# State space tables from compact operands, rotation first, one latent normalization later in the list, and a shorter exponential polynomial

## Chip, cores and metric

The kernel runs on one core of a Trainium2 chip. The metric is the device time of one execution in microseconds (us), the median of several runs. TensorE (PE in the rows) multiplies matrices, VectorE (DVE), ScalarE (ACT) and GpSimd (POOL) work on elements, and SyncE (SP) issues nearly all transfers. Each engine takes its instructions strictly in the order of its own queue, so an instruction that waits holds up everything behind it on that engine.

## What is computed

A trunk of two layers over 256 tokens of width 1024. Each layer has three token mixers in parallel (RWKV-7, latent attention, a diagonal state space model called S5), a gated merge, and a SwiGLU feed-forward network, each followed by a layer norm. The change touches the S5 parameters, which depend on the weights alone:

```python
step = exp(log_step); mag = exp(lam_re * step); ang = lam_im * step
lb_re, lb_im = mag * cos(ang), mag * sin(ang)          # lambda
f_re, f_im = (lambda - 1) / lam                        # complex
bb = f * b                                             # complex, 32 groups x 64 states x 16 channels
bu = einsum('btgc,gpc->btgp', ug, bb)
s  = associative_scan(lambda, bu)                      # over 256 positions
y  = Re(einsum('btgp,gcp->btgc', s, c)) + d_skip * u
```

and the normalization of the two latent vectors of the attention, `rms_norm(c_q)` and `rms_norm(c_kv)`, of layer 0.

## The kernel before

All projections are computed in three passes of a split format: each weight chunk (128 x 1024 fp32) is loaded by SyncE into a tile `raw` (3 buffers), cast by ScalarE to its high part (`whi`, line 161), and VectorE computes the low part (`wlo`, line 171; for a few chunks GpSimd does the last columns, line 173). There are 4 buffers of each part, and four chunks are kept ahead of the one in use. A projection unit uses two chunks: 48 matmuls on lines 203 to 205.

The work of a layer's first stage is written as a list of tokens, `ORDER1`. For layer 0: `S0 S1` are the S5 input projections, `m` the latents, `P` parameter loads, `r0` to `r6` the RWKV projections, `G1 to G3` gate projections, `T0 T1 T2` the parts of the S5 tables, `N` the latent normalization (`mla_norm`, lines 619 to 651), `t0` to `t3` with `w0` to `w3` the four S5 tiles, `g0 g1` the activation after them. The list order is not the queue order: a scheduler of the framework puts every instruction into its engine's queue by its own estimate of when its operands are there, and uses the list as a priority. So an instruction of a late token can stand early in a queue when an engine would otherwise be free.

The S5 scalars come from line 262 on, on VectorE in tiles of 128 x 32: `exp_acc` (line 275) evaluates an exponential with 24 instructions, and is called for `step` and for the magnitude. Sine and cosine come from ScalarE (lines 309, 310).

`s5_tables` (line 348) is a generator in three parts:
- T0 (to the first `yield`): loads of `pb` (line 362, the B operand) and `cd` (line 376, the C operand) from `in_spB`, in which the host has stored them already spread to block-diagonal form, half zeros. Then three complex products `cmul` (lines 379 to 386, six instructions of 128 x 512 each): B times f, B times lambda, C times minus conjugate lambda, and a negation (line 394).
- T1: 32 transposes of `bd` into `bl` (line 404) and 32 small matmuls for `k0` (line 413).
- T2: the rotation tables `ct` and `st` (lines 421 to 435), cos and sin of n times the angle for 128 steps, by doubling: 12 blocks of six instructions, from 128 x 16 elements each up to 128 x 512.

In layer 0 the products run on VectorE and the rotation on GpSimd (`TE_ = "VG"`). The tables of layer 1 are made during the first feed-forward matmuls of layer 0, all on GpSimd, at the units f = 7, 12 and 17 (`TAB_AT`).

An S5 tile (`s5_tile`, line 693) multiplies a matmul result (line 702, weights `bl`) with `ct` and `st` on VectorE (lines 709 to 712), scans (line 721), multiplies again (lines 725 to 727), and finishes on TensorE (lines 735 to 747).

The normalization `N` squares and sums on ScalarE (lines 624, 625), adds the epsilon on VectorE (line 235), takes the power -1/2 on GpSimd (line 237, tile `rsm`), and scales on ScalarE (lines 630, 631):

```python
def rsqrt(out, in_, eps, E=V):
    if eps:
        E.tensor_scalar(out=out, in0=in_, scalar1=eps, scalar2=None, op0=ALU.add)
        in_ = out
    G.tensor_tensor(out=out, in0=in_, in1=mh(out), op=ALU.pow)
```

After the feed-forward matmuls of layer 0 comes `token_major` (line 474), which loads `lg`, `lb` and `xk` (lines 493 to 495) into memory that the temporary tiles of `s5_tables` held before.

Of the kernel before, what the change touches and what calls it, by code (L numbers as in the profile page):

```python
# [26 lines left out]
    "S0 m S1 P r0 T0 T1 r1 N T2 r2 t0 w0 r3 G3 t1 t2 w1 r4 r5 w2 t3 w3 g0 G1 r6 G2 g1",  # L27
# [6 lines left out]
TAB_AT = (7, 12, 17)  # L34
# [52 lines left out]
def trunk(ctx: ExitStack, tc: tile.TileContext, xT, xtok, ws, spA, spB, spC, sp5, lnv, cst, out, dbg=None,  # L87
# [181 lines left out]
    with tc.tile_pool(name="s5set", bufs=1) as q:  # L269
# [78 lines left out]
    def s5_tables(l, tab, tmp, G, E):  # L348
# [12 lines left out]
        pb = tmp.tile([128, 2, 8, 2, 32], F32, name="pb", tag="pb")  # L361
        SY.dma_start(out=pb, in_=spB[l, :, 0:1024].rearrange("p (r q a c) -> p r q a c", r=2, q=8, a=2))
# [8 lines left out]
        G.tensor_tensor(out=st[:, :, 0], in0=cc, in1=cc, op=ALU.add)  # L371

        bd = tmp.tile([128, 8, 2, 2, 2, 32], F32, name="bd", tag="bd")
        bt = tmp.tile([128, 8, 2, 32], F32, name="bt", tag="bt")
        cd = tab.tile([128, 4, 8, 2, 32], F32, name="cd", tag="cd")
        SY.dma_start(out=cd[:, 0:2], in_=spB[l, :, 1024:2048].rearrange("p (r q a c) -> p r q a c", r=2, q=8, a=2))
        sh4 = [128, 8, 2, 32]

        def cmul(o_re, o_im, fr, fi, x_re, x_im):
            fr, fi = bc(v2(fr, 8).unsqueeze(3), sh4), bc(v2(fi, 8).unsqueeze(3), sh4)  # L380
            G.tensor_tensor(out=o_re, in0=x_re, in1=fr, op=ALU.mult)
            G.tensor_tensor(out=bt, in0=x_im, in1=fi, op=ALU.mult)
            G.tensor_tensor(out=o_re, in0=o_re, in1=bt, op=ALU.subtract)
            G.tensor_tensor(out=o_im, in0=x_im, in1=fr, op=ALU.mult)
            G.tensor_tensor(out=bt, in0=x_re, in1=fi, op=ALU.mult)
            G.tensor_tensor(out=o_im, in0=o_im, in1=bt, op=ALU.add)

        def B(i, ri):
            return bd[:, :, ri, :, i]

        cmul(B(1, 0), B(1, 1), s5fr[:, p0:p0 + 16], s5fi[:, p0:p0 + 16], pb[:, 0], pb[:, 1])
        cmul(B(0, 0), B(0, 1), lr, li, B(1, 0), B(1, 1))

        G.tensor_scalar(out=cd[:, 1], in0=cd[:, 1], scalar1=-1.0, scalar2=None, op0=ALU.mult)
        G.tensor_scalar(out=li, in0=li, scalar1=-1.0, scalar2=None, op0=ALU.mult)
        cmul(cd[:, 2], cd[:, 3], lr, li, cd[:, 0], cd[:, 1])
# [3 lines left out]
        for q4 in range(4):  # L400
            ps = mxps("a")
            for qq in range(2):
                for ri in range(2):
                    PE.transpose(ps[:, 256 * qq + 128 * ri:256 * qq + 128 * ri + 128],
                                 bd[:, 2 * q4 + qq, ri].rearrange("p a i c -> p (a i c)"), ident)
# [12 lines left out]
        yield  # L418
        mark("s5pre")

        t2 = tmp.tile([128, 16, 32], F32, name="t2", tag="t2")
        n = 1
        while n < 128:
            w = min(n, 32)
            lc, ls = (bc(x[:, :, n - 1:n], [128, 16, w]) for x in (ct, st))
            for o in range(0, n, w):
                c0, s0, t = ct[:, :, o:o + w], st[:, :, o:o + w], t2[:, :, 0:w]
                c1, s1 = ct[:, :, n + o:n + o + w], st[:, :, n + o:n + o + w]
                E.tensor_tensor(out=c1, in0=c0, in1=lc, op=ALU.mult)
                E.tensor_tensor(out=t, in0=s0, in1=ls, op=ALU.mult)  # L430
                E.tensor_tensor(out=c1, in0=c1, in1=t, op=ALU.subtract)
                E.tensor_tensor(out=s1, in0=c0, in1=ls, op=ALU.mult)  # L432
                E.tensor_tensor(out=t, in0=s0, in1=lc, op=ALU.mult)
                E.tensor_tensor(out=s1, in0=s1, in1=t, op=ALU.add)  # L434
            n *= 2
# [84 lines left out]
    for l in range(layers):  # L520
# [136 lines left out]
        with tc.tile_pool(name=f"s5p{l}", bufs=1, side=P) as q:  # L657
# [831 lines left out]
```

## Time and profile before

| | |
|---|---|
| median of 3 runs | 1088.11 us (1084.67 to 1090.08) |
| the profiled execution | 1090.58 us, its span 1088.9 us |
| mean granted TensorE clock | 0.972 |
| PE busy | 1026.9 us, 94% of the span |
| DVE busy | 802.8 us, 74% |
| ACT busy | 477.3 us, 44% |
| POOL busy | 231.5 us, 21% |

A row of a timeline gives the start, the duration, the engine, the line, the operation, output and inputs, and in brackets the idle time of the engine before it with what ended it. Times are from the start of the span. Matmuls overlap, so how fast TensorE really goes is read from how many of them start in a stretch, not from the duration of one.

### The profile page before, as it was taken

How to read it: one execution, taken by the hardware profiler on the slowest of the kernel's cores; microseconds unless marked ns; L12 is line 12 of the kernel's file. 1: busy time of each engine (PE TensorE's matmuls, PEld its weight loads, DVE VectorE, ACT ScalarE, POOL GpSimd, SP SyncE). 2: the span in 40 equal slices, each digit the busy share in tenths (PEclk: the TensorE clock that was granted, in tenths of full speed). 3: DMA queues.
4: the chain of work that ended last, by engine and by line, in shares of the span. 5: the costliest groups of instructions: out<-in, count | busy, mean ns of one | idle time of the engine just before them, and what ended most of it. 6: DMA issues, size and time to landing. Idle time of an engine off the chain costs nothing.

```text
span 1088.9 us, 21216 instructions
## 1 busy us (share of the span) xinstructions
PE 1026.9 (94%) x8560; PEld 923.8 (85%) x8560; DVE 802.8 (74%) x1560; ACT 477.3 (44%) x789; POOL 231.5 (21%) x254
## 2 busy tenths in 40 slices
PE   9489999999999999899998999999999899999997
PEld 8378887888897899798878999878889779999985
DVE  7599988977478799576473898789756866676645
ACT  5243387544343344244325345765334433434331
POOL 2941042210000599400011003221002420000000
PEclk9789999999999999999998899999999999999999
DMA  7342262132285655466545325222225746555552
GB/s 279 98 140 86 95 192 73 59 118 96 81 291 183 204 173 167 178 209 217 184 143 177 115 80 173 90 97 79 79 98 169 243 152 230 186 183 180 186 195 78
DMA packets 47683, 164.91 MB, mean 151 GB/s; under 512 B 5729, under 2 KB 8289, under 8 KB 46689
## 3 DMA queue, kind: packets, MB, share of 16 engines
q1 hardware_dynamic: 47296, 163.03, 45.2%
q8 instruction: 67, 1.10, 0.4%
q10 hardware_dynamic: 288, 0.52, 0.1%
q14 instruction: 32, 0.25, 0.1%
HBM read 157.77 MB, written 4.19 MB: 149 GB/s over the span
## 4 chain that ended last, share of the span: by engine, by line
PE 61%; DVE 17%; POOL 10%; DMA 5%; ACT 3%; issue 3%; SPq 0%; DVEq 0%; ACTq 0%; POOLq 0%
PE mm L205 11%; PE mm L204 11%; PE mm L203 11%; DMA raw<-in_ws 4%; PE mm L488 3%; PE mm L489 3%; PE mm L487 3%; DVE wlo L171 3%; ACT whi L161 2%; DVE z L721 2%; POOL st L432 1%; POOL st L434 1%; PE pa L702 1%; POOL t L430 1%; PE pa L916 1%
## 5 line engine op out<-in xcount | busy, mean ns | idle before, releaser
L171 DVE TENSOR_TENSOR wlo<-raw,whi 128x1024 fp32r<-128x1024 f32 (+2 forms) x265 | 336.7, 1277 | 175.3 <-ACT whi L161 173.2
L161 ACT CAST whi<-raw 128x1024 fp32r<-128x1024 f32 (+2 forms) x267 | 277.5, 1043 | 386.0 <-PE mm L204 207.3
L203 PE MATMUL mm<-xh,whi 128*128 128x256 f32 x1312 | 379.5, 289 | 14.2 <-ACT whi L161 14.1
L205 PE MATMUL mm<-xh,wlo 128*128 128x256 f32 x1312 | 378.3, 289 | 2.1 <-DVE wlo L171 1.9
L204 PE MATMUL mm<-xl,whi 128*128 128x256 f32 x1312 | 379.3, 289 | 0.4 <-DVE xl L259 0.4
L203 PEld LDWEIGHTS mm<-xh,whi 128*128 128x128 f32 x1312 | 252.5, 192 | 18.7 <-ACT whi L161 14.7
L205 PEld LDWEIGHTS mm<-xh,wlo 128*128 128x128 f32 x1312 | 253.5, 193 | 6.1 <-DVE wlo L171 2.9
L204 PEld LDWEIGHTS mm<-xl,whi 128*128 128x128 f32 x1312 | 252.4, 192 | 3.9 <-issue 1.8
L237 POOL TENSOR_TENSOR rs<-rs,mhalf 128x1 f32<-128x1 f32 x8 | 7.8, 970 | 344.0 <-DVE rs L235 344.0
L203 PE MATMUL mm<-yh,whi 128*128 128x256 f32 x256 | 74.5, 291 | 0.1
L205 PE MATMUL mm<-yh,wlo 128*128 128x256 f32 x256 | 74.1, 290 | 0.0
L204 PE MATMUL mm<-yl,whi 128*128 128x256 f32 x256 | 74.1, 289 | 0.0
L488 PE MATMUL mm<-wlo,hh 128*128 128x512 f32 x132 | 52.0, 394 | 0.0
L487 PE MATMUL mm<-whi,hh 128*128 128x512 f32 x132 | 51.6, 394 | 0.0
L489 PE MATMUL mm<-whi,hl 128*128 128x512 f32 x132 | 51.5, 393 | 0.0
L203 PEld LDWEIGHTS mm<-yh,whi 128*128 128x128 f32 x256 | 48.5, 189 | 2.3 <-ACT qa L113 0.9
L204 PEld LDWEIGHTS mm<-yl,whi 128*128 128x128 f32 x256 | 48.5, 189 | 1.2 <-issue 0.8
L205 PEld LDWEIGHTS mm<-yh,wlo 128*128 128x128 f32 x256 | 48.6, 190 | 1.1 <-issue 0.7
L173 POOL TENSOR_TENSOR wlo<-raw,whi 128x384 fp32r<-128x384 f32 (+2 forms) x24 | 29.5, 1236 | 72.4 <-ACT whi L161 72.4
L237 POOL TENSOR_TENSOR rsn<-rsn,mhalf 128x8 f32<-128x8 f32 x4 | 6.5, 1634 | 142.8 <-DVE rsn L235 142.8
L923 POOL TENSOR_SCALAR_AFFINE_SELECT Mk<-Mk 64x512 f32<-64x512 f32 x32 | 27.0, 844 | 43.6 <-ACT Mk L113 42.3
L487 PEld LDWEIGHTS mm<-whi,hh 128*128 128x128 f32 x132 | 24.8, 188 | 6.1 <-DVE th L1260 0.7
(498 smaller groups left out, 1764.2 us busy)
## 6 DMA issues: line engine op xcount, KB each, us to landing
raw<-in_ws SPq DMA_DIRECT2D x267, 512.0 KB, 4.1
raw<-in_ws SPq DMA_DIRECT2D x8, 416.0 KB, 3.5
xd<-xk SPq DMA_DIRECT2D x3, 1024.0 KB, 4.1
xk<-xd SPq DMA_DIRECT2D x3, 1024.0 KB, 7.9
lg<-in_lnv SPq DMA_DIRECT2D x4, 512.0 KB, 5.1
lb<-in_lnv SPq DMA_DIRECT2D x4, 512.0 KB, 5.7
pc<-in_spC SPq DMA_DIRECT2D x2, 768.0 KB, 5.1
pb<-in_spB SPq DMA_DIRECT2D x2, 512.0 KB, 5.2
```

The lines of the kernel that those rows point to most:

```text
L161: S.copy(out=hi[:, s], in_=raw[:, s])
L171: V.tensor_tensor(out=lo[:, 0:m], in0=raw[:, 0:m], in1=hi[:, 0:m].bitcast(F32), op=ALU.subtract)
L173: G.tensor_tensor(out=lo[:, m:w], in0=raw[:, m:w], in1=hi[:, m:w].bitcast(F32), op=ALU.subtract)
L203: PE.matmul(ps, lhsT=wh, rhs=xh, start=first, stop=False)
L204: PE.matmul(ps, lhsT=wh, rhs=xl, start=False, stop=False)
L205: PE.matmul(ps, lhsT=wl, rhs=xh, start=False, stop=last)
L237: G.tensor_tensor(out=out, in0=in_, in1=mh(out), op=ALU.pow)
L487: PE.matmul(acc[b][n], lhsT=ah, rhs=w[0][:, s], start=(k == 0), stop=False)
L488: PE.matmul(acc[b][n], lhsT=ah, rhs=w[1][:, s], start=False, stop=False)
L489: PE.matmul(acc[b][n], lhsT=al, rhs=w[0][:, s], start=False, stop=(k == nk - 1))
L721: V.tensor_tensor_scan(out=z[:, pp, qq, ri], data0=bc(m2[:, j:j + 1], [128, 128]), data1=z[:, pp, qq, ri], initial=0.0, op0=ALU.mult, op1= ...
L923: G.affine_select(out=Mk[r, h], in_=Mk[r, h], pattern=[[0, 4], [1, 2], [1, 64]], compare_op=ALU.is_ge, fill=0.0, base=-1, channel_multipli ...
```

## The change

The host stores the B and C operands compactly (16 columns for each group, no zeros), so one load of half the size replaces two. The complex products work in place on the compact tile `pb`, with six instructions of 128 x 256; a helper `spread` then writes the block-diagonal form with two ScalarE instructions of 128 x 512, each scaled with a 0/1 column. There are four spreads, so eight ScalarE instructions for each layer. The generator has five parts now. In layer 0 the rotation stands in the first; in layer 1 it stays last. `N` of layer 0 goes from behind `r1` to behind `r5`, `t0` from behind `r2` to behind `G3`. `exp_acc` has 15 instructions in place of 24.

```diff
-    "S0 m S1 P r0 T0 T1 r1 N T2 r2 t0 w0 r3 G3 t1 t2 w1 r4 r5 w2 t3 w3 g0 G1 r6 G2 g1",
+    "S0 m S1 P r0 T0 T1 r1 T2 T3 r2 r3 T4 G3 t0 w0 r4 t1 r5 N w1 t2 w2 r6 t3 w3 g0 G1 G2 g1",
...
-TAB_AT = (7, 12, 17)
+TAB_AT = (7, 8, 9, 12, 17)
...
-            V.tensor_scalar(out=xc, in0=src, scalar1=-104.0, scalar2=88.7, op0=ALU.max, op1=ALU.min)
+            V.tensor_scalar(out=xc, in0=src, scalar1=-88.1, scalar2=88.7, op0=ALU.max, op1=ALU.min)
             V.tensor_scalar(out=n, in0=xc, scalar1=1.4426950408889634, scalar2=MAGIC, op0=ALU.mult, op1=ALU.add)
-            V.tensor_scalar(out=n, in0=n, scalar1=MAGIC, scalar2=None, op0=ALU.subtract)
-            V.tensor_scalar(out=n, in0=n, scalar1=-127.0, scalar2=127.0, op0=ALU.max, op1=ALU.min)
+            V.tensor_scalar(out=n, in0=n, scalar1=MAGIC + 127.0, scalar2=MAGIC, op0=ALU.min, op1=ALU.subtract)
...
-            V.tensor_scalar(out=r, in0=r, scalar1=-1.0, scalar2=1.0, op0=ALU.max, op1=ALU.min)
             co = [1.0 / math.factorial(k) for k in range(9)]
-            V.tensor_scalar(out=pl, in0=r, scalar1=co[8], scalar2=co[7], op0=ALU.mult, op1=ALU.add)
-            for k in range(6, -1, -1):
-                V.tensor_tensor(out=pl, in0=pl, in1=r, op=ALU.mult)
-                V.tensor_scalar(out=pl, in0=pl, scalar1=co[k], scalar2=None, op0=ALU.add)
             V.tensor_scalar(out=ni, in0=n, scalar1=127.0, scalar2=8388608.0, op0=ALU.add, op1=ALU.mult)
-            V.tensor_tensor(out=dst, in0=pl, in1=ni.bitcast(F32), op=ALU.mult)
+            V.tensor_scalar(out=pl, in0=r, scalar1=co[8], scalar2=None, op0=ALU.mult)
+            for k in range(7, 0, -1):
+                V.scalar_tensor_tensor(out=pl, in0=pl, scalar=co[k], in1=r, op0=ALU.add, op1=ALU.mult)
+            V.scalar_tensor_tensor(out=dst, in0=pl, scalar=1.0, in1=ni.bitcast(F32), op0=ALU.add, op1=ALU.mult)
...
-        pb = tmp.tile([128, 2, 8, 2, 32], F32, name="pb", tag="pb")
-        SY.dma_start(out=pb, in_=spB[l, :, 0:1024].rearrange("p (r q a c) -> p r q a c", r=2, q=8, a=2))
+        pb = tmp.tile([128, 4, 8, 2, 16], F32, name="pb", tag="pb")
+        SY.dma_start(out=pb, in_=spB[l].rearrange("p (r q a c) -> p r q a c", r=4, q=8, a=2))
...
+        def rotation():
...
+        if first:
+            rotation()
+            yield
...
-        SY.dma_start(out=cd[:, 0:2], in_=spB[l, :, 1024:2048].rearrange("p (r q a c) -> p r q a c", r=2, q=8, a=2))
...
+        def cmul(x, fr, fi):
+            fr, fi = (bc(v2(t, 8).unsqueeze(3), [128, 8, 2, 16]) for t in (fr, fi))
+            G.tensor_tensor(out=bs, in0=x[:, 0], in1=fi, op=ALU.mult)
+            G.tensor_tensor(out=bt, in0=x[:, 1], in1=fi, op=ALU.mult)
+            G.tensor_tensor(out=x[:, 0], in0=x[:, 0], in1=fr, op=ALU.mult)
+            G.tensor_tensor(out=x[:, 1], in0=x[:, 1], in1=fr, op=ALU.mult)
+            G.tensor_tensor(out=x[:, 0], in0=x[:, 0], in1=bt, op=ALU.subtract)
+            G.tensor_tensor(out=x[:, 1], in0=x[:, 1], in1=bs, op=ALU.add)
+
+        def spread(dst, src):
+            for g in range(2):
+                S.activation(out=dst[:, :, 16 * g:16 * g + 16], in_=src.rearrange("p r q a c -> p (r q a) c"),
+                             func=AF.Identity, scale=C(f"g{g}"))
...
+        cmul(pb[:, 0:2], s5fr[:, p0:p0 + 16], s5fi[:, p0:p0 + 16])
+        spread(bdv[:, :, 1], pb[:, 0:2])
+        G.tensor_scalar(out=pb[:, 3], in0=pb[:, 3], scalar1=-1.0, scalar2=None, op0=ALU.mult)
+        spread(cd[:, 0:2].rearrange("p r q a c -> p (r q a) c"), pb[:, 2:4])
+        yield
+        cmul(pb[:, 0:2], lr, li)
+        spread(bdv[:, :, 0], pb[:, 0:2])
+        yield
         G.tensor_scalar(out=li, in0=li, scalar1=-1.0, scalar2=None, op0=ALU.mult)
-        cmul(cd[:, 2], cd[:, 3], lr, li, cd[:, 0], cd[:, 1])
+        cmul(pb[:, 2:4], lr, li)
+        spread(cd[:, 2:4].rearrange("p r q a c -> p (r q a) c"), pb[:, 2:4])
         yield
...
+        if not first:
+            yield
+            rotation()
```

In the diff `G` is the engine that `s5_tables` is given for the products: VectorE in layer 0, GpSimd in layer 1. The first call passes `first=True`, the second `False`.

## Rows read from the trace of the kernel before

**Rows 1.** The page: TensorE and its clock in 40 slices, tenths.
```profile
PE   9489999999999999899998999999999899999997
PEclk9789999999999999999998899999999999999999
```
**Rows 2.** Busy time by stretch: length, PE, PEld, DVE, ACT, POOL, PEclk, DMA share, GB/s.
```profile
34.20:46.20 12.00, 2.79 (x24) 2.58 (x22) 0.00 (x0) 1.73 (x4) 11.59 (x17) 0.76 0.01 4
46.20:67.90 21.70, 10.16 (x107) 9.09 (x108) 21.67 (x17) 5.74 (x12) 21.27 (x14) 0.66 0.32 97
...
97.00:134.00 37.00, 36.37 (x441) 32.10 (x440) 36.74 (x81) 12.97 (x20) 1.06 (x1) 1.00 0.26 88
...
36.90:71.20 34.30, 13.55 (x124) 12.39 (x124) 24.97 (x22) 8.58 (x17) 30.25 (x25) 0.65 0.21 63
455.00:470.00 15.00, 9.87 (x58) 9.37 (x58) 9.02 (x14) 6.44 (x9) 0.00 (x0) 0.77 0.73 258
...
56.90:60.70 3.80, 3.80 (x19) 3.80 (x19) 3.80 (x6) 0.47 (x1) 3.72 (x4) 0.50 0.34 130
...
380.00:400.00 20.00, 20.00 (x169) 20.00 (x169) 19.35 (x21) 8.32 (x12) 19.92 (x15) 1.00 0.58 181
```
**Rows 3.** Waits, 20 to 80 us: who waited for whom, total, times, longest.
```profile
ACT lt L630 <- POOL rsm L237: 14.6, 1, 14.6
...
PE mm L203 <- ACT whi L161: 9.3, 1, 9.3
...
PE pb L413 <- DVE bd L383: 7.3, 1, 7.3
```
**Rows 4.** Timeline of GpSimd: start of the rotation, the power, end of the rotation.
```profile
23.91 0.22 POOL L429 TENSOR_TENSOR ct<-ct 128x16 f32<-128x16 f32 x1 [3.59 <-DVE ct L369]
...
41.36 1.04 POOL L430 TENSOR_TENSOR t<-st 128x512 f32<-128x512 f32 x1
...
43.39 1.04 POOL L237 TENSOR_TENSOR rsm<-rsm,mhalf 128x4 f32<-128x4 f32 x1
...
66.25 1.61 POOL L434 TENSOR_TENSOR st<-st,t 128x512 f32<-128x512 f32 x1
```
**Rows 5.** Timeline of VectorE in layer 0's first stage.
```profile
14.10 0.19 DVE L289 TENSOR_TENSOR t5pl<-t5pl,t5r 128x32 f32<-128x32 f32 x1
14.33 0.18 DVE L290 TENSOR_SCALAR t5pl<-t5pl 128x32 f32<-128x32 f32 x1
...
65.16 1.56 DVE L383 TENSOR_TENSOR bd<-bd,bt 128x512 f32<-128x512 f32 x1
...
79.81 0.69 DVE L709 TENSOR_TENSOR pa__882<-pa,ct 128x512 f32<-128x512 f32 x1 [0.85 <-PE pa L702]
...
87.92 0.41 DVE L727 SCALAR_TENSOR_TENSOR pb<-z,st 128x256 f32<-128x256 f32 x1
```
**Rows 6.** VectorE's groups by shape, 380 to 450 us (GpSimd busy).
```profile
L171 DVE TENSOR_TENSOR wlo<-raw,whi 128x1024 fp32r<-128x1024 f32 x22 | 41.7, 1924 | 2.2 <-ACT whi L161 2.2
L1291 DVE TENSOR_TENSOR hl<-th,hh 128x256 fp32r<-128x256 f32 x11 | 12.5, 1141 | 0.4
```
**Rows 7.** The same groups, 470 to 500 us (GpSimd idle).
```profile
L171 DVE TENSOR_TENSOR wlo<-raw,whi 128x1024 fp32r<-128x1024 f32 x10 | 12.2, 1223 | 6.3 <-ACT whi L161 6.2
L1291 DVE TENSOR_TENSOR hl<-th,hh 128x256 fp32r<-128x256 f32 x6 | 2.5, 425 | 0.2
```
**Rows 8.** Timeline of GpSimd in layer 0's feed-forward stage: a step of 256, the last step.
```profile
382.23 0.61 POOL L430 TENSOR_TENSOR t<-st 128x256 f32<-128x256 f32 x1
...
447.12 2.15 POOL L434 TENSOR_TENSOR st<-st,t 128x512 f32<-128x512 f32 x1
```
**Rows 9.** SyncE's own waits, 360 to 500 us.
```profile
SPq L493 <- POOL st L434: 12.1, 1, 12.1
```
**Rows 10.** Timeline of ScalarE: a late cast, an activation with a column operand.
```profile
459.02 1.04 ACT L161 CAST whi<-raw 128x1024 fp32r<-128x1024 f32 x1 [13.99 <-DMA raw<-in_ws]
...
635.61 0.72 ACT L762 ACTIVATE ga<-ga,ones 128x512 f32<-128x512 f32 x1
```

More of the change, by code (lines that the diff above doesn't have):

```diff
@@ L346, in step, with s5_tables @@
             next(g)
-    def s5_tables(l, tab, tmp, G, E):
+    def s5_tables(l, tab, tmp, G, E, first):
         mark("s5pre")
@@ L371, in s5_tables @@
         G.tensor_tensor(out=st[:, :, 0], in0=cc, in1=cc, op=ALU.add)
-        bd = tmp.tile([128, 8, 2, 2, 2, 32], F32, name="bd", tag="bd")
-        bt = tmp.tile([128, 8, 2, 32], F32, name="bt", tag="bt")
-        cd = tab.tile([128, 4, 8, 2, 32], F32, name="cd", tag="cd")
-        SY.dma_start(out=cd[:, 0:2], in_=spB[l, :, 1024:2048].rearrange("p (r q a c) -> p r q a c", r=2, q=8, a=2))
[L377 to L394, printed above, removed]
+        def rotation():
+            mark("s5pre")
+            t2 = tmp.tile([128, 16, 32], F32, name="t2", tag="t2")
+            n = 1
+            while n < 128:
+                w = min(n, 32)
+                lc, ls = (bc(x[:, :, n - 1:n], [128, 16, w]) for x in (ct, st))
+                for o in range(0, n, w):
+                    c0, s0, t = ct[:, :, o:o + w], st[:, :, o:o + w], t2[:, :, 0:w]
+                    c1, s1 = ct[:, :, n + o:n + o + w], st[:, :, n + o:n + o + w]
+                    E.tensor_tensor(out=c1, in0=c0, in1=lc, op=ALU.mult)
+                    E.tensor_tensor(out=t, in0=s0, in1=ls, op=ALU.mult)
+                    E.tensor_tensor(out=c1, in0=c1, in1=t, op=ALU.subtract)
+                    E.tensor_tensor(out=s1, in0=c0, in1=ls, op=ALU.mult)
+                    E.tensor_tensor(out=t, in0=s0, in1=lc, op=ALU.mult)
+                    E.tensor_tensor(out=s1, in0=s1, in1=t, op=ALU.add)
+                n *= 2
@@ new lines, in s5_tables @@
+        if first:
+            rotation()
+            yield
+            mark("s5pre")
+        bt, bs = (tmp.tile([128, 8, 2, 16], F32, name=n, tag=n) for n in ("bt", "bs"))
+        bd = tmp.tile([128, 2, 8, 2, 2, 32], F32, name="bd", tag="bd")
+        cd = tab.tile([128, 4, 8, 2, 32], F32, name="cd", tag="cd")
+        def cmul(x, fr, fi):
[6 more added lines that the diff above has]
+            G.tensor_tensor(out=x[:, 1], in0=x[:, 1], in1=bs, op=ALU.add)
@@ L404, in s5_tables @@
                     PE.transpose(ps[:, 256 * qq + 128 * ri:256 * qq + 128 * ri + 128],
[L405 removed]
+                                 bd[:, ri, 2 * q4 + qq].rearrange("p a i c -> p (a i c)"), ident)
             cp(0, out=bl[:, 2 * q4:2 * q4 + 2], in_=ps.rearrange("p (q r s) -> p q r s", q=2, r=2))
@@ L412, in s5_tables @@
             for ri in range(2):
-                PE.matmul(o, lhsT=bd[:, qx, ri, pp, 1], rhs=cd[:, ri, qx, pp], start=(ri == 0), stop=(ri == 1),
+                PE.matmul(o, lhsT=bd[:, ri, qx, pp, 1], rhs=cd[:, ri, qx, pp], start=(ri == 0), stop=(ri == 1),
                           skip_group_check=True)
@@ L417, in s5_tables @@
             cp(1, out=k0[r], in_=v2(ps[r, 0:256], 8))
[L418 to L435, printed above, removed]
+        if not first:
+            yield
+            rotation()
         tb.update(ct=ct, st=st, m2=m2, cd=cd, bl=bl, k0=k0)
@@ L677, in s5_tables0 @@
                     tmps = ExitStack()
-                    tgen.append((tmps, s5_tables(0, tab, tmps.enter_context(tc.tile_pool(name="tmp0", bufs=1, side="right")), TE[0], TE[1])))
+                    tgen.append((tmps, s5_tables(0, tab, tmps.enter_context(tc.tile_pool(name="tmp0", bufs=1, side="right")), TE[0], TE[1], True)))
                 next(tgen[0][1])
-                if i == 2:
+                if i == 4:
                     tgen[0][0].close()
@@ L1293, in trunk @@
                     if f == TAB_AT[0]:
-                        gen = s5_tables(l + 1, tab, tmpq, G, G)
+                        gen = s5_tables(l + 1, tab, tmpq, G, G, False)
                     next(gen)
-                    if f == TAB_AT[2]:
+                    if f == TAB_AT[-1]:
                         tmpstack.close()
@@ L1439, in cb @@
             return a.reshape(16, 2, 16, 64).transpose(1, 3, 0, 2).reshape(128, 16, 16)
-        def diag(a):
-            o = np.zeros((2, 64, 16, 2, 16), np.float32)
-            for i in range(2):
-                o[i, :, :, i, :] = a.reshape(2, 64, 16, 16)[i]
-            return o.reshape(128, 512)
         cr, ci = cb(g["s5_c_re"][l]), cb(g["s5_c_im"][l])
-        spB.append(np.concatenate([diag(a) for a in (br, bi, cr, ci)], 1))
+        spB.append(np.concatenate([a.reshape(128, 256) for a in (br, bi, cr, ci)], 1))
     lre = np.concatenate([pg_(g["s5_lambda_re"][l]) for l in range(nl)], 1)
```

3 lines of the change are left out of this document (added).

## Prediction

> **What bounds the kernel now.** The page comes first: in its 40 slices TensorE shows nearly full digits everywhere but in the second (4, with the clock at 7), and 8 in the third, the 17th and the 22nd [rows 1]. The 22nd is the start of layer 1, which the change leaves as it is. So a gain has to come from the holes in the second and third and in the 17th slice; elsewhere a faster side engine buys nothing.
>
> The first hole is read by stretches [rows 2]. From 36.9 to 71.2 us TensorE is busy 13.6 of 34.3 us at a granted clock of 0.65, a mix of its two levels. From 34.2 to 46.2 VectorE does nothing at all, while GpSimd works 11.6 of 12 us. The waits name the chain [rows 3]: ScalarE stands 14.6 us at the scaling of the latents, behind the power on GpSimd; the weight casts queue behind it, so TensorE stands 9.3 us, then 7.3 us more for the table products, which VectorE could only start late. The power is one short instruction, but it stands in the middle of the rotation [rows 4]: GpSimd begins at 23.9, reaches the power at 43.4, and finishes the rotation at 67.9.
>
> The second hole is at 455 to 470 us. SyncE waits 12.1 us with its load of the norm's `lg` until GpSimd has finished the last step of layer 1's rotation at 449.3 [rows 8, 9], because that memory is still in use. Weight loads queue behind it; ScalarE then waits 14 us for a chunk [rows 10]. TensorE starts 58 matmuls in 15 us [rows 2]. At the upper clock level it starts one every 0.12 us (169 in 20 us) and at the lower one every 0.20 (19 in 3.8) [rows 2], so those 58 are 7 us of work: about 8 us are lost.
>
> **A shared resource.** A VectorE instruction with two operands in SBUF is lengthened while GpSimd runs, by a nearly fixed amount: 128 x 256 goes from 0.43 to 1.14 us, 128 x 1024 from 1.22 to 1.92 [rows 6, 7], and 128 x 512 from 0.69 in the S5 tile to 1.56 in a product [rows 5]. GpSimd's own step of 512 goes from 1.04 to 1.61 [rows 4]. From 46.2 to 67.9 the two take turns, 17 instructions against 14 [rows 2]. So I count the first hole as one shared queue: undisturbed, the 14 GpSimd steps are 14 x 1.04 = 14.6 us, and VectorE's 17 are about 11.0 (11 products at 0.69, two low parts at 1.15, four small ones); the sum, 25.6, took 21.7 us, a factor of 0.85. This matters: ending VectorE's 12 us of idleness does not bring 12 us, since GpSimd used that time undisturbed.
>
> **Polynomial.** Each call loses 9 of 24 instructions, which follow each other every 0.23 us [rows 5]: 2.1 us for each. The first sits before the rotation, so it starts at about 21.9, not 23.9; the second sits before the first product, so the products too can start about 2 us earlier. By the Vector Engine (DVE) Microarchitecture Reference of the Trainium skill (Points that are easy to get wrong) a scalar_tensor_tensor with two wide SBUF sources runs at half throughput; this would make each of the 16 new steps about 0.03 us longer and cost 0.5 us of the 4. The rows disagree: at 128 x 256 this form takes 0.41 us [rows 5], the plain one 0.43 [rows 7], so I leave it out.
>
> **Layer 0, products and rotation.** From 32.2 us on (34.2 less 2) GpSimd has left what it did in 34.2 to 46.2 without the power, 10.6 us, and 14.6 us: 25.2. VectorE must bring, up to the state that it had reached at 79.8, when the first S5 tile began [rows 5]: 18 products of 128 x 256 at 0.42 (7.6), a negation (0.3), seven low parts (8.0), six token-shift steps (2.8): 18.7. The sum 43.9 x 0.85 = 37.3, so rotation, products and seven chunks are done at 69.5: 10.3 us before the old 79.8. TensorE has to follow: four units (r1, r2, r3, G3) of 48 matmuls, and by estimate 3 us for the transposes and `k0`, from 36.9 on. At 0.12 us a matmul that ends at 63, at 0.20 at 78; half of each gives 71. I take 71 for t0, a gain of 9 us, bounds 0 (lower clock throughout) and 17 (upper clock, no turn-taking). From 97 to 134 both VectorE and TensorE are nearly full [rows 2], so the gain is carried on, not won again.
>
> **Spreads, loads and the moved step.** A spread is two activations at 0.72 us [rows 10], eight in each layer, 5.8 us. ScalarE is busy 5.7 of 21.7 us in the first hole [rows 2], so they fit; without that cover they cost 5.8. What they may cost as a wait is a rival below. The second load, of `cd`, goes: half a megabyte less, counted as nothing, as the DMA engines are at 0.32 or less in the first hole [rows 2]. `N` moved: its ScalarE instructions, five small VectorE steps, the power and eight transposes go behind r5; its results are first read after 134, so nobody waits, and GpSimd is nearly idle there (1.1 of 37 us [rows 2]). Its VectorE steps have no cover there, as they had none at their old place: zero net. GpSimd's share of low parts for r4 queues behind the rotation until about 69: no loss, as r4 follows t0.
>
> **Feed-forward stage of layer 0.** There the 18 products are GpSimd's. Undisturbed, a step of 256 takes 0.61 us [rows 8] and one of 512 takes 1.04 [rows 4]; the disturbance by VectorE is added to both alike, so 18 x 0.43 = 7.7 us go, and the rotation ends at 441.5, not 449.3. If SyncE comes to `lg` at 437 as now, its wait is 4 us and the hole is nearly gone: 8 us. If the planner moves that load up by as much as GpSimd gets shorter, little is won: 1. Below: a cast is made three chunks ahead (72 matmuls, 8.6 us), less 1.05 for itself [rows 10] and 1.9 for the low part [rows 6]: a cover of 5.7 us. A spread may wait for a whole chain of six products, 6 x (0.61 + 0.57) = 7.1 us, where 0.57 is what 1.61 exceeds 1.04 by [rows 4]: 1.4 too much, four times, and VectorE, full in that stage [rows 2], cannot catch up: minus 6. Between 8 and minus 6 I take plus 4, nearer to the upper end, because that hole is measured and the waits are not.
>
> **Sum.** 9 + 4 = 13 us. Against the profiled execution, 1090.6 (span 1088.9 and 1.7 around it), that is 1077.6; it lies 2.5 above the median of the runs, 1088.1, so the median goes to 1075.
>
> **Rivals.**
> 1. *The gap closes more fully* (0.20): the turn-taking costs TensorE nothing since the low parts come in time. For it: TensorE alone needs only 26 us of the 34 after 36.9, and some 21 are idle. Against: the lengthening of every two-operand instruction [rows 6, 7]. 17 + 8 = 25 us: 1063.
> 2. *The change does not do what it says* (0.15): the queue is the planner's, and the rotation already came first on GpSimd while it was last in the list [rows 4]; the power may slip again into a gap of the rotation, and ScalarE may stand again until about 41. Then VectorE begins at 44.2 with 14.6 + 18.7 = 33.3, x 0.85 = 28.3, ready at 72.5: 7 us in place of 10, still better since the products are shorter. With TensorE's clock 6 + 4: 1078.
> 3. *The wait changes its name* (0.11): ScalarE stands at the first spreads of layer 0 as it did at the scaling, each behind six products at 1.46 us (0.42 and GpSimd's 1.04 in turn), 8.8 less 5.7 of cover, three times: 9 us, which eats the gain there; the feed-forward stage brings 1 to 3: 1086.
> 4. *Slower* (0.09): in the feed-forward stage the planner sets the spreads early in ScalarE's queue, where GpSimd is late as it was 12.1 us late for `lg` [rows 9]. Then casts stand behind three chains of 7.1 us, less 5.7 of cover once: 16 us; the second hole stays, and the first brings 4: 1100. It decides against the change once these waits together pass 15 us (9 of gain and the cover).
>
> The forecast has 0.45. About 5.4 us (0.5%) is what a measurement of this kernel can tell from no change, so below 1082.7 is faster. Forecast and the first two rivals hold 0.80, of which 0.04 may end above that: faster 0.76, same 0.15, slower 0.09. The range from 1062 to 1087 takes in the full closing and the renamed wait, and leaves out the slower case and the far ends.
>
> **What the profile would show.** Right: no 14.6 us wait at line 630; VectorE idle for at most 3 us between 30 and 70; the first two-operand multiply of the S5 tile (line 709 before) at 68 to 74, not 79.8; the rotation finished near 69 with steps of 1.0 to 1.6 us; SyncE's wait for the last rotation step in the feed-forward stage under 6 us. Wrong: ScalarE waiting for a product in front of a spread for more than 5 us, with TensorE waiting for the casts behind it; the lower clock through 37 to 70; or the S5 tile as late as before because the rotation, now always in turn with VectorE, ends after 75.

## The result, and the profile after the change

The changed kernel takes 1103.32 us (median of 4 runs, 1101.64 to 1104.65) against 1086.39 us of the kernel before beside it (4 runs): a ratio of 1.0166, 95% interval 1.0138 to 1.0194. It is slower by 16.9 us where 13 us of gain were forecast. The profiled execution took 1101.64 us, its span 1099.7, the mean granted clock 0.969. Ratios here and below leave out one execution, of e5, which took 3274.92 us, three times as long as the others (its median, 1094.72, counts it and is 1093.52 without).

The page comes first, TensorE and its clock in 40 slices (answering to [rows 1]; a slice is 27.5 us here):

```profile
PE   8659989999999969999999999999999999999997
PEclk9869999999999979999999699999999999999998
```

The first hole is still there, in the second and third digits (6 and 5, the clock at 8 and 6). The hole of the 17th slice is gone, but the 15th (385 to 412 us) now holds a 6 with the clock at 7. To put times on this, three marks are read off GpSimd's timeline in every profile of this study: A is the first power on `rsn` (250.14 us before), by which the attention and RWKV work of layer 0 is well under way; B is the first copy into `lr`, where layer 1's tables begin; C is the first power of the norm after the feed-forward matmuls of layer 0. Where the end of layer 0's stage is spoken of, the first MEMSET of `qa` is meant, at 134.0 us before and 137.4 after: 3.4 of the 5.2 us that A is later are there already. Each mark comes from one profile of each kernel. Where layer 0 is the same, A differs by up to 2.4 us (247.0 in e5, 249.4 in e6), and from the stage's end to A it is 116.1 us before, 117.9 after and 121.1 in e8; so 2 or 3 us at A alone decide nothing.

| us | A | A to B | B to C | C to the end |
|---|---|---|---|---|
| before | 250.1 | 117.4 | 186.4 | 534.9 |
| changed | 255.3 | 117.8 | 197.5 | 529.1 |
| difference | +5.2 | +0.4 | **+11.1** | -5.8 |

The first three add up to 16.7 us, which is the difference of the medians. The last column is left out of this sum: it lay between 523.0 and 534.9 us in the 14 profiles of this study, and the profiled execution of before is at its upper end (that execution was itself 4.2 us above the median here). That no part of it belongs to the change is not shown: before and the two runs built on it, e4 and e8, have 529.7 to 534.9, the changed kernel and the ten built on that 523.0 to 530.9. The 6 of the clock's 23rd slice lies in it.

**Layer 0.** The stretches of [rows 2] once more (length, PE, PEld, DVE, ACT, POOL, PEclk, DMA share, GB/s):

```profile
34.20:46.20 12.00, 10.95 (x92) 10.74 (x90) 9.73 (x15) 4.61 (x8) 11.61 (x14) 1.00 0.66 205
46.20:67.90 21.70, 1.18 (x4) 0.89 (x4) 3.54 (x6) 6.18 (x12) 19.22 (x18) 0.57 0.00 0
36.90:71.20 34.30, 12.73 (x88) 12.23 (x87) 12.80 (x17) 8.64 (x16) 28.20 (x29) 0.68 0.24 75
```

The hole has moved later and become deeper. From 34.2 to 46.2 TensorE and VectorE now work, and then TensorE starts 4 matmuls in 21.7 us, where it started 107. The waits between 20 and 110 us name the same chain as [rows 3]:

```profile
PE mm L203 <- ACT whi L161: 21.1, 1, 21.1
ACT lt L647 <- POOL rsm L237: 20.7, 1, 20.7
DVE kr__236 L588 <- ACT kr__236 L587: 20.0, 2, 18.2
```

ScalarE stands at the scaling of the latents for 20.7 us, where it was 14.6. GpSimd's timeline shows why (answering to [rows 4]; the rotation is on lines 381 to 386 now):

```profile
22.30 0.28 POOL L381 TENSOR_TENSOR ct<-ct 128x16 f32<-128x16 f32 x1 [1.74 <-DVE ct L367]
...
58.66 1.25 POOL L386 TENSOR_TENSOR st<-st,t 128x512 f32<-128x512 f32 x1
59.87 1.04 POOL L237 TENSOR_TENSOR rsm<-rsm,mhalf 128x4 f32<-128x4 f32 x1
...
64.55 1.26 POOL L386 TENSOR_TENSOR st<-st,t 128x512 f32<-128x512 f32 x1
```

The rotation starts 1.6 us earlier, where 2.0 were forecast, but the power stands at 59.87 us, where it was at 43.39: behind 44 of the rotation's 48 steps, where it stood behind 33. (The rotation is 8 blocks of six steps, by the code and by the timelines; the 12 blocks of the section on the kernel before, and the 49 steps that the expectation of e3 and that of e7 name, are miscounts.) `N` was put behind `r5` in the list, and yet its power and its scaling still stand here, ahead of the casts on ScalarE. From 37.1 to 65.2 us ScalarE casts nothing, TensorE gets no weights, and the first two-operand multiply of the S5 tile starts at 89.21 us, not 79.81.

**Feed-forward stage of layer 0.** ScalarE's timeline, with the idle time before an instruction and what ended it in brackets:

```profile
376.44 1.05 ACT L161 CAST whi<-raw 128x1024 fp32r<-128x1024 f32 x1 [3.04 <-PE mm L204]
389.30 1.33 ACT L411 ACTIVATE bd<-pb,c 128x512 f32<-128x512 f32 x2 [11.80 <-POOL pb L406]
...
398.14 0.72 ACT L411 ACTIVATE bd<-pb,c 128x512 f32<-128x512 f32 x1 [5.07 <-POOL pb L406]
...
405.56 1.33 ACT L411 ACTIVATE cd<-pb,c 128x512 f32<-128x512 f32 x2 [5.13 <-POOL pb L406]
```

Three spreads wait for GpSimd, 22 us in all. What GpSimd does in the first of these waits:

```profile
373.11 0.77 POOL L356 COPY lr<-xh 128x16 f32<-128x16 f32 x1 [10.52 <-PE mm L1289]
...
375.73 0.22 POOL L381 TENSOR_TENSOR ct<-ct 128x16 f32<-128x16 f32 x1
...
384.98 0.61 POOL L382 TENSOR_TENSOR t<-st 128x256 f32<-128x256 f32 x1
385.55 0.62 POOL L401 TENSOR_TENSOR bs<-pb,s5fi 128x256 f32<-128x256 f32 x1
...
388.55 0.72 POOL L406 TENSOR_TENSOR pb<-pb,bs 128x256 f32<-128x256 f32 x1
```

It begins at 373.11, after a wait of 10.5 us that ends with a matmul of TensorE (before it was 10.5 us too), only 4.4 us before ScalarE comes to the spread, and 26 small rotation steps (375.73 to 385.55, 9.8 us) stand ahead of the first product, though the rotation is the last part of layer 1's list. The products themselves are as short as forecast, 0.62 to 0.72 us. In stretches of 24 us:

```profile
376.00:400.00 24.00, 17.82 (x126) 17.10 (x125) 5.45 (x8) 6.68 (x10) 23.25 (x47) 0.86 0.19 62
400.00:424.00 24.00, 19.29 (x122) 18.37 (x123) 17.60 (x16) 8.49 (x12) 23.73 (x18) 0.79 0.35 110
424.00:448.00 24.00, 23.20 (x193) 23.00 (x193) 21.53 (x30) 10.86 (x15) 4.75 (x4) 1.00 0.66 203
448.00:472.00 24.00, 23.85 (x252) 23.29 (x251) 14.01 (x23) 11.04 (x16) 0.00 (x0) 1.00 0.73 257
```

Before, the four counts of TensorE were 203, 203, 247 and 133:

```profile
376.00:400.00 24.00, 24.00 (x203) 24.00 (x202) 22.22 (x26) 10.18 (x13) 23.69 (x22) 1.00 0.56 178
400.00:424.00 24.00, 24.00 (x203) 24.00 (x202) 23.61 (x24) 9.94 (x13) 24.00 (x17) 1.00 0.55 173
424.00:448.00 24.00, 23.22 (x247) 22.66 (x246) 22.71 (x22) 9.99 (x15) 23.53 (x16) 1.00 0.35 118
448.00:472.00 24.00, 18.87 (x133) 18.37 (x132) 11.04 (x19) 7.07 (x9) 1.26 (x1) 0.86 0.72 246
```

In the first two it now starts 158 matmuls fewer, an estimated 19 us at 24 / 203 = 0.118 us each; in the last two 65 more, 8 us: the hole of SyncE's wait for `lg` [rows 9] is gone, because the rotation now ends at 429 us and not at 449. Net 11 us, which is the +11.1 of the table.

### The profile page after: what moved, and what is told of

Same layout as the page of the kernel before. It is cut to its first block, busy times and chain, and to the rows that moved or that the text cites. A ratio compares the mean times of both kernels' runs of the same rounds, so it can differ in the third digit from the quotient of the medians.

```text
span 1099.7 us, 21213 instructions
## 1 busy us (share of the span) xinstructions
PE 1027.0 (93%) x8560; PEld 923.5 (84%) x8560; DVE 774.7 (70%) x1542; ACT 486.8 (44%) x805; POOL 204.5 (19%) x254
## 4 chain that ended last, share of the span: by engine, by line
PE 62%; DVE 16%; POOL 8%; DMA 6%; ACT 5%; issue 3%; SPq 0%; DVEq 0%; ACTq 0%; POOLq 0%
PE mm L205 12%; PE mm L204 12%; PE mm L203 12%; DMA raw<-in_ws 6%; PE mm L505 3%; PE mm L506 3%; DVE wlo L171 3%; PE mm L504 3%; ACT whi L161 3%; DVE z L738 1%; PE pa L719 1%; PE pa L933 1%; POOL st L384 1%; PE pb L1028 1%; POOL t L382 1%
## 5 line engine op out<-in xcount | busy, mean ns | idle before, releaser
L171 DVE TENSOR_TENSOR wlo<-raw,whi 128x1024 fp32r<-128x1024 f32 (+2 forms) x265 | 326.9, 1238 | 184.2 <-ACT whi L161 180.7
L505 PEld LDWEIGHTS mm<-wlo,hh 128*128 128x128 f32 x132 | 24.8, 188 | 6.0 <-DVE wlo L171 0.6
```

The source lines that it names most:

```text
L171: V.tensor_tensor(out=lo[:, 0:m], in0=raw[:, 0:m], in1=hi[:, 0:m].bitcast(F32), op=ALU.subtract)
L505: PE.matmul(acc[b][n], lhsT=ah, rhs=w[1][:, s], start=False, stop=False)
```

## Experiments

All ratios are to the kernel before, run beside them on the same chip, so a ratio is not the quotient by the 1086.39 us above. The marks A and B to C say where a difference lies; A to B was 116.9 to 119.4 us everywhere.

**e1, layer 1's spreads on GpSimd**

```diff
-                S.activation(out=dst[:, :, 16 * g:16 * g + 16], in_=src.rearrange("p r q a c -> p (r q a) c"),
-                             func=AF.Identity, scale=C(f"g{g}"))
+                o, i = dst[:, :, 16 * g:16 * g + 16], src.rearrange("p r q a c -> p (r q a) c")
+                if first:
+                    S.activation(out=o, in_=i, func=AF.Identity, scale=C(f"g{g}"))
+                else:
+                    E.tensor_scalar(out=o, in0=i, scalar1=C(f"g{g}"), scalar2=None, op0=ALU.mult)
```

> The changed kernel, but the four spreads of layer 1 are eight multiplications on GpSimd instead of eight activations on ScalarE. Theory A (ScalarE's queue stands at the spreads: the three waits of 11.8, 5.1 and 5.1 us in the feed-forward stage of layer 0 cost some 19 us, of which the vanished wait for lg gives 8 back): the waits at the spreads are gone, TensorE is full from 380 to 420 us, and the kernel is 15 to 19 us faster than the changed one, 1083 to 1088; of before, ratio 0.998 to 1.003. Theory B (TensorE lags there for another reason, for instance VectorE lengthened by the earlier products on GpSimd, which this leaves as they are): no more than 3 us faster than the changed one, about 1100. Under both the first stage of layer 0 still ends 3 to 4 us later than before.

Measured: 1090.59 us, ratio 1.0033 (1.0007 to 1.0059). A 255.4 as in the changed kernel, B to C 188.2, 9.3 us less. TensorE is full from 380 to 420 (169 starts in each 20 us). Theory A holds in its mechanism: the waits at the spreads are gone. But the eight multiplications keep GpSimd longer, and the old hole is back.

```profile
SPq L513 <- POOL st L386: 15.5, 1, 15.5
```

SyncE waits 15.5 us for the rotation's last step; from 460 to 480 us TensorE starts only 80 matmuls. Less was won than theory A had (15 to 19 us): the median is 12.7 us below the changed kernel's. So this stage has two different losses, the spreads' waits and the wait for `lg`, and this run changes one for the other.

**e2, the spreads one part later**

```diff
-TAB_AT = (7, 8, 9, 12, 17)
+TAB_AT = (5, 8, 10, 12, 17)
...
+            gc = [C("g0"), C("g1")]
+            if not first:
...
+                gc = [gt[:, g:g + 1] for g in range(2)]
+                for g in range(2):
+                    S.activation(out=gc[g], in_=tb["th"][:, 0:1], func=AF.Identity, scale=0.0, bias=C(f"g{g}"))
...
-                             func=AF.Identity, scale=C(f"g{g}"))
+                             func=AF.Identity, scale=gc[g])
...
         yield
         mark("s5pre")
+        if not first:
+            spread(bdv[:, :, 1], pb[:, 0:2])
+            spread(cd[:, 0:2].rearrange("p r q a c -> p (r q a) c"), pb[:, 2:4])
         cmul(pb[:, 0:2], lr, li)
```

> The changed kernel with layer 1's spreads left on ScalarE, but each one part of the generator later than its products and tied to a feed-forward unit's tanh through its scale column, and the first part two units earlier (5, 8, 10, 12, 17). Theory A (only the place in ScalarE's queue is wrong): the waits of ScalarE at the spreads fall below 1 us and the kernel is 15 to 19 us faster than the changed one, 1083 to 1088. Theory B (the spreads' own 5.8 us on ScalarE, or the products on GpSimd, cost the time): little gain, 1095 to 1101.

Measured: 1080.95 us, ratio 0.9946 (0.9922 to 0.9971): faster than before. A 255.9, B to C 181.9, 15.5 us less than changed and 4.5 less than before. One wait of 3.6 us at a spread is left (theory A had under 1 us), the ties wait 4.0 us in three parts, and SyncE waits 1.9 us at `lg`, for a spread. Theory A, then: neither ScalarE's 5.8 us of spreads nor the products cost the time, but where the spreads stand in its queue. The median fell by 22.4 us, more than theory A's 15 to 19; of that the marks place only the 15.5 in this stage, and what gave the rest is open.

**e12, only the units of e2**

```diff
-TAB_AT = (7, 8, 9, 12, 17)
+TAB_AT = (5, 8, 10, 12, 17)
```

> The changed kernel with nothing but the units at which layer 1's parts stand in the list, (5, 8, 10, 12, 17) as in e2 and not (7, 8, 9, 12, 17); the spreads stay right behind their products and have no tie. It separates the two things that e2 did. Theory A (what counts is that a spread can't come to ScalarE's head before its products are done): the spreads still stand early in the queue, the waits stay at 10 to 22 us together, 1097 to 1103. Theory B (the room between the parts was enough): the waits fall below 5 us and the kernel is near e2, 1081 to 1086.

Measured: 1100.91 us, ratio 1.0157 (1.0118 to 1.0197); A 254.9, B to C 198.2, and the waits are 11.8, 5.1 and 5.1 us as in the changed kernel. The room between the parts does nothing by itself. What gives the gain of e2 is that each spread stands one part later and is held there by the tie; which of these two is needed was not tried apart.

**e3, the power early**

```diff
-    "S0 m S1 P r0 T0 T1 r1 T2 T3 r2 r3 T4 G3 t0 w0 r4 t1 r5 N w1 t2 w2 r6 t3 w3 g0 G1 G2 g1",
+    "S0 m S1 P r0 N T0 T1 r1 T2 T3 r2 r3 T4 G3 t0 w0 r4 t1 r5 w1 t2 w2 r6 t3 w3 g0 G1 G2 g1",
...
+                if first and n == 8:
+                    G.tensor_copy(out=t2[:, 0, 0:4], in_=tb["rsm"].rearrange("p a b -> p (a b)"))
```

> The changed kernel with the latent normalization ahead of the tables in the list, and the rotation's fourth doubling tied to the result of its power by a copy of 128 x 4 into the rotation's scratch tile, so that the power goes after 20 steps of the rotation and not after 49. Theory A (the power's place in GpSimd's queue sets the first hole): ScalarE's wait of 20.7 us at the scaling falls below 3 us, the first stage of layer 0 ends at 123 to 129 us where it is 137.4 now, and the kernel is 8 to 14 us faster than the changed one, 1089 to 1095. Theory B (the hole is GpSimd's and VectorE's shared work, so it stays when the power comes early): the rotation ends after 75, and the stage ends at 134 or later, 1098 or more.

Measured: 1095.60 us, ratio 1.0076 (1.0046 to 1.0105). The power is at 32.27, ScalarE waits 4.6 us, and A is 251.4, only 3.9 us less than changed; layer 0's stage ends at 133.3 (theory A: 123 to 129, theory B: 134 or later). Between the two theories: the hole is smaller, but most of the forecast gain is missing. The copy had landed on VectorE (in layer 0 that is what `G` stands for inside the tables), which stood 4.1 us at it.

**e5, the same with the copy on GpSimd**

```diff
-                    G.tensor_copy(out=t2[:, 0, 0:4], in_=tb["rsm"].rearrange("p a b -> p (a b)"))
+                    E.tensor_copy(out=t2[:, 0, 0:4], in_=tb["rsm"].rearrange("p a b -> p (a b)"))
```

> As e3, but the small copy that ties the rotation to the power runs on GpSimd: in e3 it fell to VectorE, which stood 4.1 us at it. Theory A (that stall and its delay of the products are why e3 gave 4 us and not 10): VectorE waits for nothing over 2 us between 28 and 45, the stage of layer 0 ends at 127 to 130 us (137.4 changed, 133.3 in e3), and the kernel is 8 to 11 us faster than the changed one, 1091 to 1094. Theory B (products and rotation lengthen each other, 1.26 us in place of 0.42, and that takes the rest): the stage ends at 132 to 134, within 2 us of e3.

Measured: 1094.72 us, ratio 1.0095 (1.0060 to 1.0129); A 247.0, the stage ends at 130.9, again between the two. VectorE's timeline shows what takes the rest:

```profile
42.81 0.41 DVE L405 TENSOR_TENSOR pb<-pb,lr 128x256 f32<-128x256 f32 x1
43.15 1.26 DVE L406 TENSOR_TENSOR pb<-pb,lr 128x256 f32<-128x256 f32 x1
...
47.60 2.30 DVE L171 TENSOR_TENSOR wlo<-raw,whi 128x1024 fp32r<-128x1024 f32 x1
...
51.04 1.30 DVE L406 TENSOR_TENSOR pb<-pb,lr 128x256 f32<-128x256 f32 x1
```

A product of 0.41 us takes 1.26 to 1.30 beside the rotation's large steps, and a low part 2.30; the casts and low parts queue behind. On ScalarE this is a wait for a token-shift step (`kr`) in VectorE's queue and one at a spread, and no cast between 41.9 and 57.4 us:

```profile
50.33 0.47 ACT L589 ACTIVATE kr__236<-mm,dv 128x256 f32<-128x256 f32 x1 [6.01 <-DVE kr__236 L590]
...
56.17 1.33 ACT L413 ACTIVATE cd<-pb,c 128x512 f32<-128x512 f32 x2 [3.88 <-DVE pb L408]
57.41 1.03 ACT L161 CAST whi<-raw 128x1024 fp32r<-128x1024 f32 x1
```

**e7, only the list order of e3**

```diff
-    "S0 m S1 P r0 T0 T1 r1 T2 T3 r2 r3 T4 G3 t0 w0 r4 t1 r5 N w1 t2 w2 r6 t3 w3 g0 G1 G2 g1",
+    "S0 m S1 P r0 N T0 T1 r1 T2 T3 r2 r3 T4 G3 t0 w0 r4 t1 r5 w1 t2 w2 r6 t3 w3 g0 G1 G2 g1",
```

> The changed kernel with N alone set ahead of the tables in the list, without any tie: the planner then has the power behind 34 steps of the rotation, not 49. Theory A (what counts is how many steps of the rotation stand ahead of the power): the power at 46 to 50 us instead of 59.9, ScalarE's wait 8 to 12 us instead of 20.7, the stage of layer 0 ends 2 to 4 us earlier, 1098 to 1101. Theory B (N's own instructions moved ahead cost as much as they bring): no gain, 1102 to 1105.

Measured: 1100.65 us, ratio 1.0158 (1.0124 to 1.0193). The power comes at 41.69, behind 33 steps of the rotation, and ScalarE's wait is 14.2 us, but the stage ends at 140.7 and A is 258.8, later than in the changed kernel. So theory A falls, though 1100.65 lies in its range: fewer steps ahead of the power, a ratio within the changed kernel's interval, and no gain. Again ScalarE stands for VectorE's queue, with no cast from 51.0 to 68.0 us:

```profile
63.07 0.47 ACT L587 ACTIVATE kr__236<-mm,dv 128x256 f32<-128x256 f32 x1 [9.91 <-DVE kr__236 L588]
```

**e4, the shorter polynomial alone in the kernel before** (the new `exp_acc` of the change, nothing else)

> The kernel before with the shorter exponential alone. Theory A (the first hole is set by GpSimd's chain from the rotation's start over the power): the rotation starts about 1.6 us earlier, the power and the first S5 tile with it, 0 to 2 us faster than before, 1085 to 1087. Theory B (the polynomial's rounding of the queue order moves the power elsewhere): a change of over 3 us in either direction, with ScalarE's wait at the scaling changed by as much.

Measured: 1091.90 us, ratio 1.0051 (1.0025 to 1.0077): slower. Nine vector instructions fewer in each of two calls cost some 5 us: 5.4 between the medians (before beside it took 1086.47), 5.9 at A (256.1 where it was 250.1), 3.0 at the stage's end. Theory B:

```profile
71.73 1.04 POOL L237 TENSOR_TENSOR rsm<-rsm,mhalf 128x4 f32<-128x4 f32 x1
```

The rotation starts at 22.39 instead of 23.91, and the whole of it now stands ahead of the power; ScalarE waits 22.7 us at the scaling.

**e9, the changed kernel with the old polynomial** (the old `exp_acc`, nothing else)

> The changed kernel with the old, longer exponential (24 instructions). Theory A (e4: the shorter polynomial alone, by starting the rotation earlier, moves the power deeper into it): the power stands behind 34 steps of the rotation instead of 44, at 48 to 52 us instead of 59.9, ScalarE's wait is 8 to 13 us instead of 20.7, the stage of layer 0 ends 3 to 6 us earlier, and the kernel takes 1096 to 1100. Theory B (the list order, rotation ahead of N, pushed it): the wait stays at about 20 us and the kernel is at 1102 to 1106, the polynomial's own 2 to 4 us worse.

Measured: 1098.11 us, ratio 1.0120 (1.0067 to 1.0172). The power comes at 46.71 and the wait is 13.5 us, near theory A's range; but the stage ends at 138.4 and A is 256.6, no earlier than changed. The time lies in theory A's range, but its interval and the changed kernel's overlap. ScalarE's timeline after the power:

```profile
47.78 0.51 ACT L651 ACTIVATE lt<-lt,rsm 128x256 f32<-128x256 f32 x1 [13.52 <-POOL rsm L237]
...
59.62 1.33 ACT L415 ACTIVATE bd<-pb,c 128x512 f32<-128x512 f32 x2 [5.41 <-DVE pb L410]
```

What is saved at the power is lost again at the spreads, whose products now run beside the large rotation steps. With e7 this says that the power's place alone does not set the time of layer 0: between 40 and 66 us either ScalarE stands at the power and the rotation runs undisturbed, or VectorE and GpSimd hold each other up and ScalarE stands for VectorE.

**e8, the kernel before with the power early** (the tie of e5)

> The kernel before, with the rotation tied to the power as in e5 and nothing else. Theory A (the 14.6 us wait at the scaling is worth as much in the old kernel): ScalarE's wait falls below 5 us and the kernel is 3 to 8 us faster than before, ratio 0.992 to 0.997. Theory B (the prediction's view that GpSimd and VectorE are one shared queue there, so that undoing VectorE's idle time only moves work): within 2 us of before.

Measured: 1083.25 us, ratio 0.9973 (0.9944 to 1.0002). ScalarE's wait falls from 14.6 to 6.3 us, but in the profiled execution A is even 3.6 us later (253.7), and the time cannot be told from no change. The interval holds theory B and also the upper end of theory A's range (0.9944 to 0.997), so this run does not decide between them; that the rotation now ends at 75.2 us, not at 67.9, speaks for theory B, the prediction's shared queue.

**e10, the large rotation steps behind the products**

```diff
-        def rotation():
+        def rotation(n, end, after=None):
...
+            if after is not None:
+                E.tensor_copy(out=t2[:, 0, 0:4], in_=after)
+            while n < end:
...
         if first:
-            rotation()
+            rotation(1, 16)
             yield
...
             yield
-            rotation()
+            rotation(1, 128)
+        else:
+            rotation(16, 128, pb[:, 3, 0, 0, 0:4])
```

The list order is the changed kernel's.

> The changed kernel with the rotation cut in two in layer 0: the first four doublings stay in the first part, the rest comes in the last part and is tied by a copy of 128 x 4 to the last complex product. The power then has a free GpSimd, and the products run on VectorE without the rotation beside them. Theory A (two costs in layer 0, the power's place and products lengthened by the rotation, are both gone): ScalarE waits under 4 us at the scaling, the products stay at 0.4 to 0.7 us, the stage of layer 0 ends at 125 to 129 us (137.4 changed, 130.9 in e5), 1089 to 1094. Theory B (the rotation has to be done by about 70, and later it holds up the S5 tiles): the rotation ends at 73 or later, VectorE waits for GpSimd at the first S5 tile, the stage ends at 131 or later.

Measured: 1086.51 us, ratio 0.9997 (0.9961 to 1.0034). A is 241.7, 13.6 us less than changed and 8.4 less than before; the stage ends at 122.5, below theory A's range. B to C is 197.8, as it must be with the spreads left. The power, the tie and the last product, and the stretch of [rows 2]:

```profile
39.45 1.22 POOL L237 TENSOR_TENSOR rsm<-rsm,mhalf 128x4 f32<-128x4 f32 x1
...
43.77 0.19 POOL L375 COPY t<-pb 128x4 f32<-128x4 f32 x1 [3.09 <-DVE pb L407]
```

```profile
43.29 0.41 DVE L407 TENSOR_TENSOR pb<-pb,bs 128x256 f32<-128x256 f32 x1
...
72.35 0.69 DVE L729 TENSOR_TENSOR pa__971<-pa,ct 128x512 f32<-128x512 f32 x1 [1.20 <-POOL ct L384]
```

```profile
36.90:71.20 34.30, 29.36 (x270) 28.41 (x269) 23.44 (x29) 20.25 (x34) 30.50 (x26) 0.90 0.43 133
```

270 matmuls start in a stretch where it was 124 before and 88 after the change. The power has no tie here and comes behind 26 steps, and ScalarE does not wait at the scaling at all. Theory B has a small part: the rotation ends at 74.8, and the S5 tile waits 1.2 and 1.8 us for it.

**e6 and e11, both holes**: e5 with e2, and e10 with e2.

> e5 and e2 together: power early in layer 0, spreads of layer 1 late. If the two holes are independent, the gains add: e2's 24 us and e5's 4 to 11 us from the changed kernel's 1103, so 1068 to 1076, ratio of before 0.983 to 0.991. If the second hole hides behind the first (a rival), no more than e2 gave: 1079 to 1083.

Measured: 1075.13 us, ratio 0.9912 (0.9882 to 0.9941); A 249.4, B to C 181.9. The time lies within the 1068 to 1076 that were expected if the gains add, and by the marks the feed-forward stage gives 15.5 us here as in e2.

> e10 and e2 together. If the gains add as in e6: e10's time less 20 to 24 us, 1066 to 1073, ratio of before 0.981 to 0.988. If e10 wins nothing over e5 in layer 0: 1075, as e6.

Measured: 1072.06 us, ratio 0.9860 (0.9815 to 0.9905), the fastest version here; A 243.4, B to C 180.7. That is 14.5 us less than e10, where 20 to 24 were expected of e2's part; the time lies in the expected 1066 to 1073 only because e10 was itself faster than expected. By the marks the stage gives 17.1 (197.8 to 180.7). So the two stages' gains add, but e2's gain between medians, 22.4, does not come again. Its page has no digit under 7 between the first slice and the last:

```profile
PE   9979889999999999999999999999999899999997
PEclk9998989999999999999998999999999999999999
```

## Why the prediction was wrong

The failed step is one assumption made twice: that an instruction stands in its engine's queue where the list puts it.

**Layer 0 (forecast 9 us of gain, measured 5.2 us of loss).** The sum started from a rotation without the power in it, since `N` was to "go behind r5; its results are first read after 134, so nobody waits". It did not go: its sums of squares are again done by 28 us, ScalarE comes to its scaling at 40.3 us, ahead of the casts, and the power went deeper into the rotation. That was rival 2, with 0.15. Its mechanism is seen, but its price was taken from the old place ("until about 41"); the power came at 59.9. Part of what moved it is the polynomial, costed at a clean gain: e4 shows that alone it costs some 5 us. But undoing it (e9), or only the list order (e7), brings nothing back at A, since the wait then changes its name: to the spreads in e9 (5.4 us twice), as rival 3 had it, and to a token-shift step of VectorE in e7 (9.9 us). The two were not undone together. (By the prediction's own numbers its lower bound was 2, 79.8 less 78, and not 0; the measured loss lies outside either.)

**The shared queue of VectorE and GpSimd.** The power's place is not all. In e5, where the power comes at 33 us and the two engines take turns as the sum had it, the total is about right: the products end at 56.1 and the rotation at 71.2, against the forecast's 69.5. But the first two-operand multiply of the S5 tile starts at 81.59 us, not at 71, and A gains only 3.1 us on before (0.7 in e6, with the same layer 0). So the 9 us are not borne out for this arrangement. What the sum left out is the order within that queue: the products and the token-shift steps behind them are what ScalarE and TensorE wait for, the rotation is needed only at the S5 tiles, so turn-taking in equal parts already delays the chain that counts, three products' time for one (1.26 us against 0.41). e10 puts the large rotation steps behind the products, and only then are 8.4 us gained at A (6.7 in e11).

**Feed-forward stage (forecast 4 us of gain, bounds +8 and -6; measured 11.1 us of loss).** The lower bound failed. It took each spread's wait as one chain of six products, 7.1 us less 5.7 of cover. The products were faster than that, but 26 rotation steps and a late start stood ahead of the first one, so the first wait alone was 11.8 us, and the three 22. That was rival 4, with 0.09: its place and mechanism are seen, its threshold (15 us of waits) was passed with 22, and its 1100 us is nearest to the result; only that the `lg` hole stays was wrong there. It went, since GpSimd's work in this stage shrank by more than the forecast's 7.7 us: from the first copy to the rotation's last step it takes 55.9 us, and 59.2 in e2, where VectorE does not stand, against 81.7 before. With the spreads held back (e2, e6, e11) the stage gains 4.5, 4.5 and 5.7 us. That is near the term of 4, but the term was a middle between 8 and -6, so its size is partly luck.

**What was right.** The rotation's earlier start, though by 1.6 us and not 2.0, its large steps of 1.04 to 1.26 us, its end at 65.8 (forecast near 69), and the vanished wait for `lg`. The observation that would refute the forecast, ScalarE over 5 us in front of a spread, is what the profile shows. e11, in which neither queue is held up for long, is 16.0 us below before, where 13 were forecast; but its layer 0 has another order than the sum's, so it does not confirm the sum.

The Trainium skill (PSUM — Partial Sum Buffer, Engine vs sequencer instructions) calls the queues of ScalarE, VectorE and GpSimd strictly first in, first out. Every wait above agrees: a 0.5 us scaling held up the casts behind it for 20.7 us.

What is left open: by what estimate the planner chose its places; no run shows it. Nor was it tried to keep only the small rotation steps out of layer 1's first chain, or to hold a spread by its place in the list alone.

## What to carry to other kernels

Where a scheduler fills queues by its own estimates, a list order is a wish: read from the trace where an instruction really stands, and when one engine's result releases another's queue, bound the wait by everything that may stand ahead of it, not by its own chain. Making a stage faster can move such an instruction to a worse place, so a shorter computation need not give a shorter time. A data tie by a tiny instruction (0.19 us for the copy of e10) can fix the place. The two rearrangements of e11, each held by such a tie, are worth 3% between it and the changed kernel (ratios 0.986 and 1.0166).

## What was not expected of the hardware

A GpSimd step's lengthening beside VectorE is not in proportion to its size. GpSimd, then VectorE, in the changed kernel:

```profile
23.80 1.22 POOL L384 TENSOR_TENSOR st<-ct,st 128x16 f32<-128x16 f32 x1
24.98 0.24 POOL L383 TENSOR_TENSOR ct<-ct,t 128x16 f32<-128x16 f32 x1
```

```profile
23.68 1.24 DVE L171 TENSOR_TENSOR wlo<-raw,whi 128x1024 fp32r<-128x1024 f32 x1
```

A step of 16 columns takes 1.22 us when a low part of 1.24 us began 0.12 us before it, and ends 0.1 us after it; the next takes 0.24. The Trainium skill (SBUF — State Buffer, SBUF: two separate sides) says that of a VectorE instruction with two inputs in SBUF and a GpSimd instruction that reads SBUF, whichever starts first keeps the shared port for its whole instruction, and the other blocks. These rows agree. They also explain the fixed 0.7 us of the prediction's paragraph on the shared resource, which was a mean: what is added is nearly what is left of the other engine's instruction. Here 1.12 us were left and 0.98 were added (1.22 against 0.24). Small steps are also dear without that: 128 x 16 takes about 0.2 us on GpSimd, 128 x 256 takes 0.61, so 26 of them fill 9.8 us.
